# Attention scores with K's low half stored for every kv head on both partition halves

## The chip, the cores and the metric

The kernel runs on one core of a Trainium2 chip. The metric is the device time of one execution in microseconds (us), lower is better. The profile is that of one execution, taken by the hardware profiler; its times count from the start of its span.

## The reference

One transformer layer, on 1024 tokens of width 1024, in fp32: a norm, sliding-window attention with a sink, an output projection, a second norm, a gated feed-forward of width 2816, a final norm. The attention has 16 query heads in 4 groups; each group of 4 shares one kv head of 64 numbers.

```python
def sliding_window_sink_attention(h, w_in, sinks, w_out):
    B, T, _ = h.shape
    L = SWA_BLOCK                                   # 128 queries, 256 keys
    q, k, v = split_qkv(h, w_in)                    # 16, 4 and 4 heads of 64
    qb = q.reshape(B, nb, L, N_KV_HEADS, GQA_GROUP, HEAD_DIM)
    kw, vw = with_prev(k), with_prev(v)             # own block and the one before
    s = jnp.einsum('bnqhgd,bnkhd->bnhgqk', qb, kw) * (HEAD_DIM ** -0.5)
    s = s - slopes[:, :, None, None] * dist
    s = jnp.where(mask, s, -jnp.inf)
    m = jnp.maximum(jnp.max(s, axis=-1, keepdims=True), sink)
    p = jnp.exp(s - m)
    denom = jnp.sum(p, axis=-1, keepdims=True) + jnp.exp(sink - m)
    o = jnp.einsum('bnhgqk,bnkhd->bnqhgd', p / denom, vw)
    return o.reshape(B, T, ATTN_Q_DIM).astype(h.dtype) @ w_out

x = x + swa(rms_norm(x, norm_mix));  x = x + swiglu_ffn(rms_norm(x, norm_ffn), ...)
return rms_norm(x, final_norm)
```

## The kernel before

TensorE multiplies in fp32r. To keep fp32's precision each operand is split into a high part (a rounded copy, made on ScalarE) and a low part (the rest, by a subtraction on VectorE or GpSimd), and a product is made of three: high by high, high by low, low by high. `split` (L58) writes both parts; the class `Weights` loads each weight tile into one of 3 `raw` buffers, splits it into one of 3 `wc` buffers, and loads the next when a `raw` buffer comes free. Its two instructions have the lines L60 and L63 wherever they are called.

The order of every engine's instructions is written out by hand; the framework adds the waits. The stages are these:

1. Norm and V (L313 to L430): 8 tiles of 128 tokens are normed and transposed into H; V is projected as `pv` (L370). Its weights come as two raw halves that `wv_hi` and `wv_lo` split. In between, the first two K projections start.
2. K and Q of the first 512 tokens: ten products `pc` of 24 matmuls each (L265). `evac` of the two K products writes the high part KH for kv head 2i+par on the 64 partitions of par, and a DMA (L296) copies it to the other 64, so that KH stands on both halves. The low part KL (L295) stands once, two kv heads to a tile, each on its own half. Q's high and low parts go through DRAM into `qt`: for an even kv head the high part on partitions 0 to 63 and the low part on 64 to 127, for an odd one the other way round.
3. Attention: 32 units, one for each block n of 128 queries and each kv head. `att_iter` runs four units in a pipeline, a stage each: `scores` of unit i, `transpose` and `split_p` of unit i-1, `values` and `store_hi` of unit i-2, `store_lo` of unit i-3. Between these pieces it runs steps of a stream of plain matmuls: K and Q of the second 512 tokens for units 0 to 15 (15 a unit), the output projection `mo` of the first 512 (L612, 12 a unit) for units 16 to 31.
4. The output projection of the second half, the second norm with its row `wbc` (the norm's weights on every partition), and from 414 us the feed-forward.

A unit's scores are 8 matmuls, two for each of the 4 query heads, in pairs of this form (L480 to L483):

```python
nc.tensor.matmul(ps[:, i], self.qt[:, g], KH[:, kv, win], start=True, stop=False)
nc.tensor.matmul(
    ps[:, i], self.qt[self.rows, g], KL[self.rows, self.p, win], start=False, stop=True
)
```

The first contracts over 128 partitions (both Q parts by KH), the second over the 64 of `self.rows` (Q's high part by KL). VectorE then adds the bias and takes the row maximum (L488, four times; L492 negates two maxima at a time), ScalarE takes the exponentials (L497), GpSimd scales by the reciprocal of L508 (L510, four times), TensorE transposes (L519), ScalarE and VectorE split the transposed probabilities (`pr`, L60 and L63), TensorE multiplies by V (L533), and VectorE writes the low part of the result (L550, L551). All of a unit's PSUM tiles come from one pool of 4.

Of the kernel before, what the change touches and what calls it, by code (L numbers as in the profile page):

```python
# [9 lines left out]
F32 = mybir.dt.float32  # L10
F32R = mybir.dt.float32r
# [5 lines left out]
P = 128  # L17
# [15 lines left out]
def trunk_kernel(  # L33
# [21 lines left out]
    def f(ap):  # L55
        return ap.bitcast(F32)
# [14 lines left out]

    ident = const.tile([P, P], F32, name="ident")
    small = const.tile([P, 2 + NH], F32, name="small")
    wbc = const.tile([P, D], F32, name="wbc")
    sink_bc = small[:, 2:]
    H = [hpool.tile([P, 2, 2, NK, 2 * P], F32R, name=f"H{i}") for i in range(2)]
    q_dram = [[dram.tile([P, 4, G, P], F32, name=f"qs_{i}_{kv}") for kv in range(NKV)] for i in range(2)]
# [51 lines left out]
                lo = slot[:, 1, 4 * b : 4 * b + 4, off : off + P]  # L129
                split(hi, lo, self.pts[b], nc.scalar, nc.vector)  # L130

    # ------------------------------------------------- weights, split ahead of use
    class Weights:
        def __init__(self):
            self.jobs, self.nl, self.ns, self.lo = [], 0, 0, {}
# [92 lines left out]
            add_gu(c + 2)  # L228
            add_gu(c + 3)

    # ------------------------------------------------------------ matmul streams
    class Stream:
        def __init__(self, gen):
            self.gen, self.late, self.done = gen, [], False
# [38 lines left out]
    kvpool_cm = tc.tile_pool(name="kvpool", bufs=1)  # L273
    kvpool = kvpool_cm.__enter__()
    KH = kvpool.tile([P, NKV, T], F32R, name="KH")
    KL = kvpool.tile([P, 2, T], F32R, name="KL")
    VV = kvpool.tile([P, NT, 2, 4, HD], F32R, name="VV")
    qs_cm = tc.tile_pool(name="qs", bufs=2, side="right")
    qs = qs_cm.__enter__()
# [1 line left out]
    def qkv_steps(half):  # L281
        for i in range(10):
            ts_ = slice(half * 512, half * 512 + 512)
            j = half * 10 + i
            wc = W.get(j)
            ps = psg.tile([P, 512], F32, tag="g", name=f"pc_{half}_{i}")

            def evac(i=i, ps=ps, ts_=ts_):
                if i < 2:
                    for par in range(2):  # L290
                        r = slice(par * HD, par * HD + HD)
                        r2 = slice((1 - par) * HD, (1 - par) * HD + HD)
                        kv = 2 * i + par
                        nc.scalar.activation(KH[r, kv, ts_], ps[r], AF.Copy)
                        nc.vector.tensor_tensor(KL[r, i, ts_], ps[r], f(KH[r, kv, ts_]), ALU.subtract)  # L295
                        nc.sync.dma_start(f(KH[r2, kv, ts_]), f(KH[r, kv, ts_]))  # L296
                    return
                kv, gp = (i - 2) // 2, (i - 2) % 2
                qst = qs.tile([P, 2, 4, P], F32R, tag="qst", name=f"qst_{half}_{i}")
                pv = ps.rearrange("p (n q) -> p n q", n=4)  # L300
                nc.scalar.activation(qst[:, 0], pv, AF.Copy, scale=HD**-0.5)
                nc.vector.scalar_tensor_tensor(qst[:, 1], pv, HD**-0.5, f(qst[:, 0]), ALU.mult, ALU.subtract)
                for gi in range(2):
                    src = f(qst[gi * HD : (gi + 1) * HD])
                    for hl in range(2):
                        row = hl if kv % 2 == 0 else 1 - hl
                        dst = q_dram[half][kv][row * HD : (row + 1) * HD, :, gp * 2 + gi]
                        nc.sync.dma_start(dst, src[:, hl])

            yield from gemm_steps(ps, wc, half, lambda j=j: W.want(j + 3), evac)  # L310

    # ------------------------------------------------------- norm, V, first half
    early_cm = tc.tile_pool(name="early", bufs=1)  # L313
    early = early_cm.__enter__()
    manual = tc.manual_schedule()
# [4 lines left out]
    def load_x(t):  # L320
        xts[t] = early.tile([P, D], F32, tag="x", name=f"x_{t}", bufs=4)
        nc.sync.dma_start(xts[t], x[t * P : (t + 1) * P, :])

    row = early.tile([1, D], F32, name="row")
    srow = early.tile([1, NH], F32, name="srow")
    wv = early.tile([P, 2, NK, 256], F32R, name="wv")
    wv_raw = early.tile([P, NK, 256], F32, name="wv_raw")

    def load_wv(k2):
        nc.sync.dma_start(  # L330
            wv_raw[:, 4 * k2 : 4 * k2 + 4],
            w_in[k2 * 512 : k2 * 512 + 512, 1280:1536].rearrange("(k p) n -> p k n", p=P),
        )

# [17 lines left out]

    def wv_hi(k2):
        s = slice(4 * k2, 4 * k2 + 4)
        nc.scalar.activation(wv[:, 0, s], wv_raw[:, s], AF.Copy)

    def wv_lo(k2, eng):
        s = slice(4 * k2, 4 * k2 + 4)
        eng.tensor_tensor(wv[:, 1, s], wv_raw[:, s], f(wv[:, 0, s]), ALU.subtract)

    vps = {}

# [23 lines left out]
        norms[t].scale(**k)  # L386

    n_scale(0, halves=True)
    nc.vector.tensor_copy(wv[:, 0, :4], wv_raw[:, :4])
    norms[0].apply(parts=2)  # L390
    load_x(4)
    norms[0].transpose()
# [36 lines left out]
        v_evac(t)  # L429
    early_cm.__exit__(None, None, None)  # L430

    # ---------------------------------------------------------------- attention
    att_cm = tc.tile_pool(name="att", bufs=2)
    att = att_cm.__enter__()
    bias = att.tile([P, NH, 2 * P], F32, name="bias", bufs=1)
# [19 lines left out]
    class Unit:  # L455
# [12 lines left out]
        def scores(self):  # L468
            n, kv, b0, key = self.n, self.kv, self.b0, self.key
            w0 = max(n - 1, 0) * P  # L470
            win = slice(w0, w0 + 2 * P)
            nw = 2 * P - b0
            self.tt = att.tile([P, G, 2 * P], F32, tag="t", name=f"t_{key}", bufs=3)
            self.st = att.tile([P, 6, G], F32, tag="st", name=f"st_{key}", bufs=4)
            st = self.st
            for gp in range(2):
                ps = psa.tile([P, 2, 2 * P], F32, tag="a", name=f"s_{key}_{gp}")
                for i in range(2):
                    g = gp * 2 + i
                    nc.tensor.matmul(ps[:, i], self.qt[:, g], KH[:, kv, win], start=True, stop=False)  # L480
                    nc.tensor.matmul(  # L481
                        ps[:, i], self.qt[self.rows, g], KL[self.rows, self.p, win], start=False, stop=True
                    )  # L483
                gs = slice(gp * 2, gp * 2 + 2)
                for i in range(2):
                    g = gp * 2 + i
                    h = kv * G + g
                    nc.vector.tensor_tensor_reduce(  # L488
                        self.tt[:, g, b0:], ps[:, i, :nw], bias[:, h, b0:], scale=1.0,
                        scalar=sink_bc[:, h : h + 1], op0=ALU.add, op1=ALU.max, accum_out=st[:, 0, g : g + 1],  # L490
                    )
                nc.vector.tensor_scalar(st[:, 1, gs], st[:, 0, gs], -1.0, None, ALU.mult)  # L492
# [53 lines left out]
        def store_lo(self):  # L546
            slot = o_slot(self.n, self.p)
            rows, orow = self.rows, self.orow
            ot = att.tile([P, G, P], F32, tag="ot", name=f"ot_{self.key}", bufs=2)
            nc.vector.tensor_tensor(ot[rows], self.po[rows], f(slot[rows, 0]), ALU.subtract)  # L550
            nc.vector.tensor_tensor(slot[rows, 1], ot[rows], self.po[orow], ALU.add)  # L551

# [138 lines left out]
    s3 = Stream(out1_steps())  # L691
    for i in range(32, 35):
        att_iter(i, s3, 12)
    nc.sync.dma_start(wbc, norm_ffn[0].partition_broadcast(P))
    x2_cm.__exit__(None, None, None)
    att_cm.__exit__(None, None, None)
    kvpool_cm.__exit__(None, None, None)

    # ------------------------------------- output projection of the second half
    accp = ctx.enter_context(tc.tile_pool(name="accp", bufs=1))  # L700
    acc = [accp.tile([P, D], F32, name=f"acc_{t}") for t in range(NT)]
    xp = ctx.enter_context(tc.tile_pool(name="xp", bufs=2))
    actp = ctx.enter_context(tc.tile_pool(name="actp", bufs=3))
    wo1_cm = tc.tile_pool(name="wo1", bufs=1)
# [18 lines left out]
    s3.finish()  # L723
    wo1_cm.__exit__(None, None, None)

    # -------------------------------------------------------------------- ffn
    dnp = ctx.enter_context(tc.tile_pool(name="dnp", bufs=2))
    acts, gps = {}, {}

# [147 lines left out]
```

## Time and profile before

| | |
|---|---|
| Time, median of 3 runs | 1137.02 us (1136.62 to 1139.21) |
| Span of the profiled execution | 1136.2 us |
| TensorE busy | 1100.1 us, 97% |
| VectorE busy | 524.1 us, 46% |
| ScalarE busy | 345.9 us, 30% |
| GpSimd busy | 174.8 us, 15% |
| Attention, units 0 to 31 (scores of the first to scores of the last) | 114.6 to 341.5 us |
| Feed-forward | from 414 us to the end |

The profiled execution has no time of its own beside its span. The span lies 0.8 us under the median of the runs, and 0.4 us under the fastest: what lies around it is taken as that. A busy TensorE is one that has a matmul in flight, so 97% does not say that it works at its peak; how far apart the matmuls start does.

### The profile page before, as it was taken

The page shows a single profiled execution, that of the slowest core. Times are in us where ns is not written, and L with a number is a line of the kernel's source. Part 1 is how long each engine was busy: PE and PEld are TensorE (multiplying, and loading weights), DVE is VectorE, ACT ScalarE, POOL GpSimd, SP SyncE. Part 2 cuts the span into 40 slices and gives each one's busy share as a digit, 9 for nine tenths or more (in the row PEclk, how much of TensorE's full clock was granted, in tenths as well). Part 3 has the DMA queues.
Part 4 walks back from the last instruction along what each step waited for, and adds up shares of the span by engine and source line. Part 5 has one row for each costly group of instructions (what it writes and reads, how often), then busy time and mean ns, then how long its engine had stood idle before and what let it go on. Part 6 is the DMA issues. An engine that isn't in the chain of part 4 may idle for free.

```text
span 1136.2 us, 13051 instructions
## 1 busy us (share of the span) xinstructions
PE 1100.1 (97%) x4992; PEld 891.9 (79%) x4992; DVE 524.1 (46%) x978; ACT 345.9 (30%) x703; POOL 174.8 (15%) x260
## 2 busy tenths in 40 slices
PE   3999999999999899999999999999999999999997
PEld 2988777777777778888888888888888888888885
DVE  2544577777876634342524333242423334252427
ACT  2532566566664533111120212112020211111016
POOL 2357344444442100000000000000000000000002
PEclk6999999999999999999999999999999999999999
DMA  5257544543436613121120212121030212103003
GB/s 185 93 132 200 129 116 110 128 118 109 118 87 179 173 37 111 37 60 53 33 61 19 76 36 74 37 56 46 11 93 19 75 37 56 56 4 90 1 1 148
DMA packets 104305, 91.02 MB, mean 80 GB/s; under 512 B 4275, under 2 KB 87219, under 8 KB 104244
## 3 DMA queue, kind: packets, MB, share of 16 engines
q1 hardware_dynamic: 102946, 85.74, 27.2%
q10 hardware_dynamic: 1298, 4.46, 1.2%
q8 instruction: 39, 0.64, 0.2%
q14 instruction: 22, 0.18, 0.0%
HBM read 74.45 MB, written 14.68 MB: 78 GB/s over the span
## 4 chain that ended last, share of the span: by engine, by line
PE 93%; DMA 2%; issue 1%; ACT 1%; DVE 1%; POOL 0%; POOLq 0%; SPq 0%; ACTq 0%
PE gu L265 42%; PE d L821 21%; PE pc L265 10%; PE mo L612 5%; PE s L481 3%; PE s L480 3%; PE po L533 2%; PE pt L519 2%; DMA acc<-x2s 2%; PE pv L370 2%; PE mo L673 1%; PE pt_a L122 1%; PE pt_b L122 1%; DMA wv_raw<-in_swa_w_in_dram 0%; DVE xn_a L112 0%
## 5 line engine op out<-in xcount | busy, mean ns | idle before, releaser
L265 PE MATMUL gu<-H,wc_gu 128*128 128x512 f32 x2112 | 481.3, 389 | 0.0
L265 PEld LDWEIGHTS gu<-H,wc_gu 128*128 128x128 f32 x2112 | 396.3, 188 | 82.8
L821 PE MATMUL d<-wc_dn,act 128*128 128x512 f32 x1056 | 241.7, 390 | 0.0
L821 PEld LDWEIGHTS d<-wc_dn,act 128*128 128x128 f32 x1056 | 198.2, 188 | 41.7
L833 DVE TENSOR_TENSOR acc<-d,acc 128x512 f32<-128x512 f32 x176 | 121.6, 691 | 97.5 <-PE d L821 96.5
L63 DVE TENSOR_TENSOR wc_gu<-raw_gu,wc_gu 128x1024 fp32r<-128x1024 f32 x44 | 53.8, 1223 | 185.5 <-ACT wc_gu L60 185.5
L265 PE MATMUL pc<-H,wc_c 128*128 128x512 f32 x480 | 122.8, 399 | 2.2 <-POOL wc_c L63 2.2
L785 POOL TENSOR_SCALAR ssq_f<-ssq_f 128x1 f32<-128x1 f32 x7 | 1.3, 192 | 710.7 <-ACT sq L784 710.7
L265 PEld LDWEIGHTS pc<-H,wc_c 128*128 128x128 f32 x480 | 87.0, 188 | 21.6 <-POOL wc_c L63 2.6
L745 DVE TENSOR_TENSOR sil<-sil,gu 128x512 f32<-128x512 f32 x44 | 30.3, 688 | 136.7 <-PE gu L265 136.7
L60 ACT ACTIVATE act<-sil 128x512 fp32r<-128x512 f32 x44 | 27.8, 633 | 201.6 <-DVE sil L745 201.6
L497 ACT ACTIVATE t<-t,st 128x256 f32<-128x256 f32 (+1 forms) x128 | 62.4, 488 | 72.4 <-DVE st L492 72.3
L60 ACT ACTIVATE wc_dn<-raw_dn 128x1024 fp32r<-128x1024 f32 x22 | 22.1, 1051 | 197.7 <-PE d L821 197.7
L612 PE MATMUL mo<-wc_o,H 128*128 128x512 f32 x288 | 78.8, 405 | 0.0
L741 ACT ACTIVATE sil<-gu 128x512 f32<-128x512 f32 x44 | 26.4, 599 | 168.5 <-PE gu L265 168.5
L488 DVE CUSTOM_DVE_ANT_0 t<-s,bias,small 128x256 f32<-128x256 f32 (+1 forms) x128 | 54.6, 463 | 32.7 <-PE s L481 32.2
L510 POOL TENSOR_SCALAR t<-t,st 128x256 f32<-128x256 f32 (+1 forms) x128 | 57.6, 471 | 56.6 <-DVE st L508 26.5
L612 PEld LDWEIGHTS mo<-wc_o,H 128*128 128x128 f32 x288 | 51.4, 188 | 11.8 <-DVE xh L641 0.4
L63 POOL TENSOR_TENSOR wc_c<-raw_c,wc_c 128x1024 fp32r<-128x1024 f32 x20 | 48.1, 2407 | 26.6 <-ACT wc_c L60 19.4
L481 PE MATMUL s<-KL,qt 64*128 64x256 f32 x128 | 48.7, 380 | 0.0
L60 ACT ACTIVATE wc_gu<-raw_gu 128x1024 fp32r<-128x1024 f32 x44 | 46.1, 1048 | 8.4 <-issue 8.4
L63 DVE TENSOR_TENSOR pr<-pt,pr 128x512 fp32r<-128x512 f32 x60 | 41.0, 688 | 12.3 <-ACT pr L60 10.8
(96 smaller groups left out, 857.8 us busy)
## 6 DMA issues: line engine op xcount, KB each, us to landing
raw_gu<-in_ffn_w_gate_up_dram SPq DMA_DIRECT2D x44, 512.0 KB, 5.0
raw_dn<-in_ffn_w_down_dram SPq DMA_DIRECT2D x22, 512.0 KB, 3.4
raw_c<-in_swa_w_in_dram SPq DMA_DIRECT2D x20, 512.0 KB, 4.0
qs<-qst SPq DMA_DIRECT2D x64, 128.0 KB, 2.5
qt<-qs SPq DMA_DIRECT2D x32, 256.0 KB, 4.0
raw_o<-in_swa_w_out_dram SPq DMA_DIRECT2D x24, 256.0 KB, 3.8
x<-in_x_dram SPq DMA_DIRECT2D x8, 512.0 KB, 3.5
out_dram<-acc SPq DMA_DIRECT2D x7, 512.0 KB, 2.6
```

The lines of the kernel that those rows point to most:

```text
L60: nc.scalar.activation(hi, src, AF.Copy)
L63: lo_eng.tensor_tensor(lo, src, f(hi), ALU.subtract)
L265: nc.tensor.matmul(ps, wc[:, wl, k], hh[:, :, hl, k, :], start=(n == 0), stop=(n == 3 * NK - 1))
L480: nc.tensor.matmul(ps[:, i], self.qt[:, g], KH[:, kv, win], start=True, stop=False)
L481: nc.tensor.matmul(ps[:, i], self.qt[self.rows, g], KL[self.rows, self.p, win], start=False, stop=True)
L488: nc.vector.tensor_tensor_reduce(self.tt[:, g, b0:], ps[:, i, :nw], bias[:, h, b0:], scale=1.0, scalar=sink_bc[:, h : h + 1], op0=ALU.add, ...
L497: nc.scalar.activation(self.tt[:, g, b0:], self.tt[:, g, b0:], AF.Exp, bias=st[:, 1, g : g + 1], accum_out=st[:, 3, g : g + 1],)
L510: nc.gpsimd.tensor_scalar(self.tt[:, g, b0:], self.tt[:, g, b0:], st[:, 2, g : g + 1], 0.0, ALU.mult, ALU.add)
L612: nc.tensor.matmul(pss[i], o[:, a, g], wt[:, b, ci], start=(c == 0 and n % 3 == 0), stop=(c == 7 and n % 3 == 2))
L745: nc.vector.tensor_tensor(sil, sil, ps, ALU.mult)
L821: nc.tensor.matmul(ps, acts[c][:, a, t * P : (t + 1) * P], dnw[c][:, b, s], start=(n == 0), stop=(n == 3 * len(cs) - 1),)
L833: nc.vector.tensor_tensor(acc[t][:, s], ps, acc[t][:, s], ALU.add)
```

## The change

The low part of K gets the layout that the high part has: `KL` holds all four kv heads, and a second DMA copies each piece to the other 64 partitions. The second matmul of each pair then contracts over 128 partitions; Q's low part by KL, which was left out, is added to the scores. `KL` doubles, so three buffers move: the norm row `wbc` becomes two tiles in pools that live shorter, `ot` has one buffer in place of two, and V's raw weights share the three `raw` buffers of the weight tiles.

```diff
@@ -71,7 +71,6 @@
-    wbc = const.tile([P, D], F32, name="wbc")
@@ -273,7 +272,7 @@
-    KL = kvpool.tile([P, 2, T], F32R, name="KL")
+    KL = kvpool.tile([P, NKV, T], F32R, name="KL")
@@ -292,8 +291,9 @@
                         nc.scalar.activation(KH[r, kv, ts_], ps[r], AF.Copy)
-                        nc.vector.tensor_tensor(KL[r, i, ts_], ps[r], f(KH[r, kv, ts_]), ALU.subtract)
+                        nc.vector.tensor_tensor(KL[r, kv, ts_], ps[r], f(KH[r, kv, ts_]), ALU.subtract)
                         nc.sync.dma_start(f(KH[r2, kv, ts_]), f(KH[r, kv, ts_]))
+                        nc.sync.dma_start(f(KL[r2, kv, ts_]), f(KL[r, kv, ts_]))
@@ -321,14 +321,15 @@
+    wbc = early.tile([P, D], F32, name="wbc_mix")
     row = early.tile([1, D], F32, name="row")
     srow = early.tile([1, NH], F32, name="srow")
     wv = early.tile([P, 2, NK, 256], F32R, name="wv")
-    wv_raw = early.tile([P, NK, 256], F32, name="wv_raw")
+    wv_raw = [wp.tile([P, 4, 256], F32, tag="raw", name=f"wv_raw_{i}", bufs=3) for i in range(2)]
@@ -478,9 +479,7 @@
                     nc.tensor.matmul(ps[:, i], self.qt[:, g], KH[:, kv, win], start=True, stop=False)
-                    nc.tensor.matmul(
-                        ps[:, i], self.qt[self.rows, g], KL[self.rows, self.p, win], start=False, stop=True
-                    )
+                    nc.tensor.matmul(ps[:, i], self.qt[:, g], KL[:, kv, win], start=False, stop=True)
@@ -546,7 +545,7 @@
-            ot = att.tile([P, G, P], F32, tag="ot", name=f"ot_{self.key}", bufs=2)
+            ot = att.tile([P, G, P], F32, tag="ot", name=f"ot_{self.key}", bufs=1)
@@ -691,14 +690,15 @@
-    nc.sync.dma_start(wbc, norm_ffn[0].partition_broadcast(P))
     x2_cm.__exit__(None, None, None)
     att_cm.__exit__(None, None, None)
     kvpool_cm.__exit__(None, None, None)
@@
     acc = [accp.tile([P, D], F32, name=f"acc_{t}") for t in range(NT)]
+    wbc = accp.tile([P, D], F32, name="wbc_ffn")
+    nc.sync.dma_start(wbc, norm_ffn[0].partition_broadcast(P))
```

On TensorE, VectorE, ScalarE and GpSimd the instructions stand in the same order as before; the queue of SyncE (SP), which issues most DMAs, gets eight more. Two places show it. A row gives the line, what is written and read, the size, and in brackets what the instruction waits for: engines by name, earlier DMAs as DMAHW.

The first place is the start of the program on SP: the loads of the first K weights (`raw_c`) and of the token tiles 4 to 7 (`x`). Before:

```order
L173 DMA raw_c_0_119<-in_swa_w_in_dram 128x8x128 [waits DMAHW0_49]
L173 DMA raw_c_1_121<-in_swa_w_in_dram 128x8x128 [waits DMAHW1_49]
L173 DMA raw_c_2_123<-in_swa_w_in_dram 128x8x128 [waits DMAHW2_49]
L322 DMA x_166<-in_x_dram 128x1024 [waits DMAHW3_49,DVE_49,Activation_49]
L322 DMA x_190<-in_x_dram 128x1024 [waits DMAHW4_49,DVE_49,Activation_49]
```

And with the change:

```order
L172 DMA raw_c_0_120<-in_swa_w_in_dram 128x8x128 [waits DMAHW0_49]
L172 DMA raw_c_1_122<-in_swa_w_in_dram 128x8x128 [waits DMAHW2_49,DMAHW1_49,Pool_49]
L172 DMA raw_c_2_124<-in_swa_w_in_dram 128x8x128 [waits DMAHW4_49,DVE_49]
L322 DMA x_167<-in_x_dram 128x1024 [waits DMAHW3_49]
L322 DMA x_191<-in_x_dram 128x1024
```

No row moved, but two of the three weight loads now wait for the engines that split V's raw weights (`wv_lo`, L359: first GpSimd, then VectorE), and the two token tiles stand behind them.

The second place is further on in the same queue, where the first K products are copied to the other partition half. Before:

```order
L173 DMA raw_c_5_401<-in_swa_w_in_dram 128x8x128 [waits DMAHW2_49,Pool_49]
L296 DMA KH<-KH 64x512 [waits Activation_49]
L296 DMA KH<-KH 64x512 [waits DMAHW3_49,Activation_49]
L173 DMA raw_c_6_486<-in_swa_w_in_dram 128x8x128 [waits DMAHW7_49,DMAHW4_49,Pool_49]
L296 DMA KH<-KH 64x512 [waits DMAHW5_49,Activation_49]
```

And with the change:

```order
L172 DMA raw_c_5_402<-in_swa_w_in_dram 128x8x128 [waits DMAHW2_49,Pool_49]
L295 DMA KH<-KH 64x512 [waits Activation_49]
L296 DMA KL<-KL 64x512 [waits DMAHW3_49,DVE_49]
L295 DMA KH<-KH 64x512 [waits DMAHW4_49,Activation_49]
L296 DMA KL<-KL 64x512 [waits DMAHW5_49,DVE_49]
L172 DMA raw_c_6_489<-in_swa_w_in_dram 128x8x128 [waits DMAHW7_49,DMAHW6_49,Pool_49]
```

Behind each copy of KH stands one of KL, which waits for VectorE's subtraction.

## Rows read from the trace of the kernel before

**Rows 1.** Windows: us, busy (instructions) of PE, PEld, DVE, ACT, POOL; PEclk, DMA.

```profile
113.00:235.00 122.00, 122.00 (x536) 89.70 (x534) 82.64 (x258) 72.32 (x207) 54.66 (x91) 1.00 0.49 118
235.00:346.00 111.00, 111.00 (x505) 82.27 (x505) 86.85 (x261) 68.77 (x199) 48.58 (x86) 1.00 0.38 106
```

**Rows 2.** The page, part 4: the chain that ended last, by engine.

```profile
PE 93%; DMA 2%; issue 1%; ACT 1%; DVE 1%; POOL 0%; POOLq 0%; SPq 0%; ACTq 0%
```

**Rows 3.** Timeline of PE, one unit's scores: start, duration (us), engine, line, operation.

```profile
303.60 0.28 PE L480 MATMUL s<-KH,qt 128*128 128x256 f32 x1
303.81 0.38 PE L481 MATMUL s<-KL,qt 64*128 64x256 f32 x1
304.12 0.38 PE L480 MATMUL s<-KH,qt 128*128 128x256 f32 x1
...
305.99 0.50 PE L612 MATMUL mo<-wc_o,H 128*128 128x512 f32 x1
```

**Rows 4.** Timeline of PEld (weight loads) in the same unit.

```profile
304.11 0.19 PEld L480 LDWEIGHTS s<-KH,qt 128*128 128x128 f32 x1
```

**Rows 5.** Timeline of PE, one tile's V projection and what follows it.

```profile
61.53 2.99 PE L370 MATMUL pv<-wv,H 128*128 128x256 f32 x24
64.35 0.39 PE L265 MATMUL pc<-H,wc_c 128*128 128x512 f32 x1
```

**Rows 6.** Tile pv: its weight loads, ns min/median/max.

```profile
L370 PEld LDWEIGHTS pv<-wv,H x192: 187/188/333, 26.2 to 84.4; 128*128 128x128 f32 x192
```

**Rows 7.** Timeline of all engines: VectorE and GpSimd around the start of that unit.

```profile
304.09 2.37 POOL L63 TENSOR_TENSOR wc_o<-raw_o,wc_o 128x1024 fp32r<-128x1024 f32 x1 [0.23 <-ACT wc_o L60]
...
304.85 0.48 DVE L488 CUSTOM_DVE_ANT_0 t<-s,bias,small 128x256 f32<-128x256 f32 x1 [1.06 <-PE s L481]
...
305.78 0.71 DVE L492 TENSOR_SCALAR st<-st 128x2 f32<-128x2 f32 x1
```

**Rows 8.** Line L492, the negated maxima: ns min/median/max.

```profile
L492 DVE TENSOR_SCALAR st<-st x64: 168/169/1357, 116.7 to 342.5; 128x2 f32<-128x2 f32 x64
```

**Rows 9.** VectorE's waits from 113 to 235: us in total, times, longest.

```profile
DVE t L488 <- PE s L481: 16.5, 19, 2.4
```

**Rows 10.** VectorE's waits from 235 to 346.

```profile
DVE t L488 <- PE s L481: 15.7, 21, 1.1
```

**Rows 11.** GpSimd's lines from 113 to 235: busy, mean ns, idle before, releaser.

```profile
L63 POOL TENSOR_TENSOR wc_c<-raw_c,wc_c 128x1024 fp32r<-128x1024 f32 x9 | 21.4, 2374 | 2.8 <-ACT wc_c L60 2.8
L63 POOL TENSOR_TENSOR wc_o<-raw_o,wc_o 128x1024 fp32r<-128x1024 f32 x2 | 4.7, 2358 | 0.7 <-ACT wc_o L60 0.7
```

**Rows 12.** GpSimd's lines from 235 to 346.

```profile
L63 POOL TENSOR_TENSOR wc_o<-raw_o,wc_o 128x1024 fp32r<-128x1024 f32 x8 | 18.9, 2366 | 2.1 <-ACT wc_o L60 2.1
```

**Rows 13.** Timeline of all engines after the attention.

```profile
355.63 0.58 SPq L694 DMA_DIRECT2D wbc<-in_norm_ffn_dram  x1
...
365.17 1.28 DVE L112 SCALAR_TENSOR_TENSOR xn_b<-acc,ssq_b,wbc 128x1024 f32<-128x1024 f32 x1 [5.87 <-DMA wbc<-in_norm_ffn_dram]
...
366.61 1.06 PE L122 MATMUL pt_b<-ident,xn_b 128*128 128x128 f32 x8 [1.34 <-DVE xn_b L112]
...
380.93 1.94 PE L122 MATMUL pt_b<-ident,xn_b 128*128 128x128 f32 x8 [3.10 <-DVE xn_b L112]
```

**Rows 14.** Windows: the stretch behind that last wait.

```profile
380.73:384.14 3.41, 3.21 (x12) 2.95 (x13) 3.41 (x6) 1.53 (x3) 0.00 (x0) 0.50 0.42 139
```

**Rows 15.** Timeline of all engines, the first stage.

```profile
28.84 1.22 DVE L359 TENSOR_TENSOR wv<-wv_raw,wv 128x1024 fp32r<-128x1024 f32 x1
...
35.11 1.06 ACT L103 ACTIVATE xn_a<-x 128x1024 f32<-128x1024 f32 x1
...
61.34 0.59 SPq L296 DMA_DIRECT2D KH<-KH  x1
```

**Rows 16.** DMA issues up to 120 us: KB each, median us to landing.

```profile
x<-in_x_dram SPq DMA_DIRECT2D x8, 512.0 KB, 3.5
...
KH<-KH SPq DMA_DIRECT2D x4, 128.0 KB, 4.3
```

More of the change, by code (lines that the diff above doesn't have):

```diff
@@ L326, in trunk_kernel @@
     wv = early.tile([P, 2, NK, 256], F32R, name="wv")
-    wv_raw = early.tile([P, NK, 256], F32, name="wv_raw")
+    wv_raw = [wp.tile([P, 4, 256], F32, tag="raw", name=f"wv_raw_{i}", bufs=3) for i in range(2)]
     def load_wv(k2):
         nc.sync.dma_start(
-            wv_raw[:, 4 * k2 : 4 * k2 + 4],
+            wv_raw[k2],
             w_in[k2 * 512 : k2 * 512 + 512, 1280:1536].rearrange("(k p) n -> p k n", p=P),
@@ L354, in wv_hi @@
         s = slice(4 * k2, 4 * k2 + 4)
-        nc.scalar.activation(wv[:, 0, s], wv_raw[:, s], AF.Copy)
+        nc.scalar.activation(wv[:, 0, s], wv_raw[k2], AF.Copy)
     def wv_lo(k2, eng):
         s = slice(4 * k2, 4 * k2 + 4)
-        eng.tensor_tensor(wv[:, 1, s], wv_raw[:, s], f(wv[:, 0, s]), ALU.subtract)
+        eng.tensor_tensor(wv[:, 1, s], wv_raw[k2], f(wv[:, 0, s]), ALU.subtract)
     vps = {}
@@ L388, in trunk_kernel @@
     n_scale(0, halves=True)
-    nc.vector.tensor_copy(wv[:, 0, :4], wv_raw[:, :4])
+    nc.vector.tensor_copy(wv[:, 0, :4], wv_raw[0])
     norms[0].apply(parts=2)
```

## The prediction

> **What bounds the kernel now.** I read the chain that ended last first: 93% of it is TensorE (PE) [rows 2]. The change touches the score matmuls, so the second view is the windows over the attention, cut where the stream of plain matmuls changes from K and Q to the output projection [rows 1]. In both stretches PE always has a matmul in flight, at a granted clock of 1.00, while VectorE (DVE) is busy for 82.64 of 122 us and 86.85 of 111 us. So PE sets the pace, but DVE is not far behind: a PE that needs a quarter less would meet it. The third view is the timeline of PE in one unit, because "in flight" does not say how fast matmuls follow each other [rows 3].
>
> **The score matmuls.** The eight matmuls of a unit take from 303.60 to 305.99, 2.39 us. After a matmul on 128 rows the one on 64 starts 0.21 later (303.60 to 303.81); the next one, on 128 rows again, starts 0.31 later (303.81 to 304.12), and the rest keep that step [rows 3]. Its weight load starts at 304.11, at the moment of its own matmul and not ahead of it [rows 4]. What does the same shape cost when all 128 rows are used every time? The trace has it: `pv` multiplies 128x128 by 128x256, the new form exactly, and its 24 matmuls run from 61.53 to 64.35 in 2.82 us, 0.118 us each [rows 5]. Their weight loads last 188 ns at the median [rows 6], longer than the step, so they must lie beside other matmuls. The step of 0.31 is then a price of the change between 128 and 64 rows, not of the load.
>
> With the change a bundle takes 8 x 0.118 = 0.94 us in place of 2.39: 1.45 less, and over 32 units 46.4 us less of PE. The multiplications that are added (64 more rows) cost nothing by the same row. The bounds for a bundle are 0.94 (as `pv`) and 2.39 (nothing gained). I take 0.94, since shape, type and order of loads are the same.
>
> The Trainium skill, "TensorE: Matmul & The Clock Gate", Part 3, says that a weight load runs beside matmuls in flight only if its row group differs from theirs. By it two matmuls on all 128 rows would load and multiply in turn and the gain would be nothing, where by the rows on `pv` it is 46.4 on PE; those rows speak against the rule, and it stands below as a rival.
>
> **What takes PE's place.** The 46.4 is a gain on PE alone. Stretch 1 (113 to 235) has 17 of the bundles, stretch 2 (235 to 346) 15. PE's floor is 122 - 17 x 1.45 = 97.4 and 111 - 15 x 1.45 = 89.3.
>
> DVE's floor starts from its busy time, 82.64 and 86.85. It idles 39.4 and 24.2, of which 16.5 and 15.7 are waits for the scores [rows 9, 10]; these go when PE is faster. The other idle time, 22.9 and 8.45, is in short waits for ScalarE and others within the pipeline.
>
> DVE's busy time does not stay, however. The negation L492 normally takes 169 ns, but up to 1357 [rows 8]. In the unit shown it takes 0.71 and ends at 306.49, just as GpSimd's split of a weight tile ends (304.09 + 2.37 = 306.46) [rows 7]. It seems held until the other engine finishes. The first reduction L488 starts at 304.85 after DVE idled 1.06 for the scores. Without that idle time L492 is due about 1.06 earlier while the split ends when it did, so it is held some 1.1 to 1.2 longer, and part of the gain is eaten. I take 1.2 for each split: 11 of them in stretch 1 (9 + 2), 8 in stretch 2 [rows 11, 12]. DVE's floor becomes 82.64 + 13.2 = 95.8 and 86.85 + 9.6 = 96.5.
>
> For stretch 1 the new length lies between 97.4 (PE's floor; DVE's is just below) and 95.8 + 22.9 = 118.7 (all other idle time kept): a gain of 3.3 to 24.6. Two engines that both are within two per cent of full can't both run without gaps; I keep a third of DVE's other idle time, 7.6, which is my choice: 103.4, a gain of 18.6. For stretch 2 the bounds are 96.5 and 104.9, a gain of 6.1 to 14.5; with a third, 2.8, it is 99.3, a gain of 11.7. If the hold on L492 does not bite, the bounds there reach PE's 89.3, a gain of 21.8.
>
> **The hand-over behind the attention.** Today PE runs late and everything else is ready. Later PE reaches the end of the attention closer to DVE, and the second norm hangs on DVE: it waits 5.87 for `wbc`, whose load is issued at 355.63, and PE waits 1.34 and then 3.10 for DVE's `xn_b` [rows 13]. What PE gained beyond the others is given back here. With four PSUM tiles PE can lead by about a unit, 233 / 32 = 7.3 us. The bounds are 0 and 7.3; I take half, 3.6.
>
> **The edits that I cost at nothing.** The eight copies of KL: SP issues a KH copy at 61.34 in 0.59 us [rows 15], so the two that follow the first K products add some 1.2 us each time to SP's queue, and a copy lands 4.3 us after its issue [rows 16]; the first scores start at 114.6. For the second half the copy of a piece runs while eight products of Q are still to come. Without that cover a copy would cost its 4.3 once in each half. V's raw weights in `raw`: the third weight load now waits for DVE's L359, which ends at 28.84 + 1.22 = 30.06 [rows 15], and token tiles 4 and 5 stand behind it in SP. Three or four issues and a landing of 3.5 us [rows 16] put tile 4 at about 34 to 36, and ScalarE reads it at 35.11 [rows 15]: 0 to 1 us late on ScalarE, and I take 0, as only the norm's next step, some microseconds on, feeds PE. If tile 4 came a whole landing later, 3.5 would be the loss. `ot` with one buffer: its writer L550 and its reader L551 follow each other on DVE, in order, so nothing waits that did not. `wbc` as two tiles: the second load now also waits for PE's last reader of the old space, the attention's last values, which are before 355.63, so nothing moves; a microsecond if not.
>
> **The sum.** The profiled execution's span is 1136.2, 0.8 below the median, and I put the differences on the median: 1137.0 - 18.6 - 11.7 + 3.6 = 1110.3. I say 1110.
>
> **The rivals.**
>
> *PE stays the only bound.* L492 is not held longer, and DVE's other waits close up. Then both stretches shrink to PE's floors: 1137.0 - 46.4 = 1090.6, up to about 1099 with the hand-over. For it: much of DVE's idle time is waiting that a new rhythm could fill. Against it: in stretch 2 DVE is busy for 86.85, against PE's 89.3, and the held L492 is plain [rows 1, 7]. Chance 0.14.
>
> *DVE takes over, with all its other waits.* The gain is 3.3 + 6.1 = 9.4, less up to 3.6 for the hand-over: 1127.6 to 1131. For it: the waits are on ScalarE's and GpSimd's work in the same chain, which is not shortened by the change. Against it: a chain over four units has slack, and a wait is shorter when DVE comes late. Chance 0.18.
>
> *The step stays at 0.31.* If the load of a 128-row matmul can't start while another one on the same rows runs, nothing is gained: load and multiplication in line take 0.19 + 0.12 = 0.31, just the step that is seen [rows 3, 4]. Then the change only swaps 0.31 for 0.31: 1137. Against it: `pv` loads and multiplies in the same way at 0.118 [rows 5, 6]. Chance 0.05. This is the rule of the Trainium skill, "TensorE: Matmul & The Clock Gate", Part 3, that was weighed above.
>
> *Slower: the clock falls in the attention.* Today PE never waits there. After the wait of 3.10 before 380.93 the granted clock in the next 3.41 us is 0.50, that is 1.2 GHz in place of 2.4 [rows 13, 14]. A PE that waits for DVE in every unit might be granted less. One such stretch does 1.7 us of full-speed work in 3.41, so it costs 1.7; with 26.7 to lose it takes 16 of them, one in every second unit, to be back at 1137, and one in each unit gives 1137 - 26.7 + 32 x 1.7 = 1165. For it: DVE's floor is close to or above PE's, so waits will come. Against it: the waits I expect sum to 6.0 (103.4 - 97.4) and 10.0 (99.3 - 89.3) us, half a microsecond a unit, well below the wait of 3.10, and single waits should stay short. Chance 0.05, most of it slower, a part within 0.3%.
>
> **How the numbers follow.** The forecast, both engines near their floors with some gaps, has a chance of 0.58 and spans 1100 to 1120. With PE alone at 1091 to 1099 (0.14) and DVE with all its waits at 1120 to 1131 (0.18) that is 0.90. The range of 1094 to 1129 leaves out 0.10 for no gain or a loss, and about 0.04 at either end of the neighbouring cases, 0.18 together. About 0.3%, 3.4 us, is what a measurement of this kernel can tell from no change. Faster by more: 0.58 + 0.14 + 0.18 = 0.90, and a little from the bundle between its bounds, 0.91; within: 0.05; slower: 0.04.
>
> **What would show it.** In the timeline of PE the score matmuls should start 0.12 apart, with weight loads ahead of their matmuls. PE should no longer be busy for 100% of the two stretches, and its waits should name DVE or the PSUM tiles that DVE frees. DVE's wait for scores should fall from 32 us to under 10, the sum of L492 should rise by some 20 us, and the stretches should measure about 103 and 99 us. The granted clock should stay at 1.00 in both. If steps of 0.31 remain, the first step is wrong; if L492's sum does not grow, the second; if PE's waits are there but behind ScalarE or GpSimd, the choice of a third. The prediction would be wrong as a whole if the clock fell in the attention, or if the start (first scores at 114.6) moved by more than a microsecond.

## The result and the profile after

The changed kernel takes 1106.43 us (median of 4 runs, 1105.46 to 1109.92) against 1137.17 us before: a ratio of 0.9734, 95% interval 0.9716 to 0.9752, 30.7 us less. The forecast was 1110, in the likeliest case, 1100 to 1120. The profiled execution has a span of 1103.7 us, 32.5 below the 1136.2 of before and somewhat more than the medians differ by.

The line of the page on the chain that ended last, by engine, shows VectorE where it had 1% before [rows 2]:

```profile
PE 81%; DVE 11%; ACT 3%; DMA 2%; issue 2%; POOL 0%; SPq 0%; POOLq 0%; DVEq 0%; ACTq 0%
```

The timeline of PE and of its weight loads (PEld) at the first bundle of scores answers to [rows 3, 4]. Both score matmuls have 128 rows, they start 0.12 apart, and a load starts with the matmul before the one that it is for:

```profile
113.57 0.28 PE L481 MATMUL s<-KH,qt 128*128 128x256 f32 x1
113.57 0.19 PEld L482 LDWEIGHTS s<-KL,qt 128*128 128x128 f32 x1
113.68 0.28 PE L482 MATMUL s<-KL,qt 128*128 128x256 f32 x1
113.69 0.19 PEld L481 LDWEIGHTS s<-KH,qt 128*128 128x128 f32 x1
113.80 0.28 PE L481 MATMUL s<-KH,qt 128*128 128x256 f32 x1
```

The windows, cut at the first scores, the first `mo`, the end of the last scores, the first `mo` of `wc_wo` and the first matmul of the feed-forward, which starts at 375.1 us here and at 407.7 in the kernel before, not at the 414 of the table ahead (the columns are those of [rows 1]):

```profile
113.60:216.70 103.10, 97.83 (x530) 80.71 (x529) 89.53 (x256) 69.55 (x206) 52.00 (x89) 1.00 0.60 143
216.70:310.30 93.60, 87.27 (x483) 71.51 (x482) 87.12 (x246) 63.54 (x189) 48.99 (x83) 1.00 0.45 124
310.30:342.60 32.30, 31.37 (x154) 25.40 (x152) 21.62 (x38) 16.40 (x30) 8.91 (x13) 1.00 0.72 196
342.60:375.10 32.50, 29.03 (x136) 23.08 (x137) 20.72 (x26) 14.47 (x24) 3.69 (x10) 0.95 0.44 130
```

The same cuts of the kernel before, taken for this comparison, are:

```profile
114.60:235.10 120.50, 120.50 (x530) 88.43 (x528) 82.74 (x258) 72.32 (x207) 54.40 (x90) 1.00 0.49 118
235.10:341.50 106.40, 106.40 (x482) 78.45 (x481) 82.55 (x249) 65.08 (x188) 47.53 (x83) 1.00 0.39 109
341.50:375.20 33.70, 31.80 (x153) 25.49 (x152) 20.89 (x33) 16.66 (x30) 8.31 (x11) 1.00 0.73 198
375.20:407.70 32.50, 29.03 (x138) 23.45 (x138) 20.80 (x26) 14.63 (x24) 3.70 (x10) 0.95 0.39 119
```

The differences are 17.4 in the first half of the attention, 12.8 in the second, 1.4 in the hand-over and nothing in the stage behind it; 1.0 lies ahead of the first scores. PE now waits: it is busy for 97.83 of 103.10 and 87.27 of 93.60 us. The waits in the first half whose last releaser is VectorE (total, times, longest) name the PSUM tiles that VectorE frees by L487, the reduction of the scores, and by its split of `pr`; VectorE hardly waits for scores any more, 1.0 us where it was 16.5 [rows 9] (the last row, from VectorE's own waits) and 1.8 in the second half, where it was 15.7 [rows 10]:

```profile
PE po L532 <- DVE st L487: 2.3, 4, 0.8
...
PE s L481 <- DVE pr L63: 1.2, 2, 0.9
...
DVE t L487 <- PE s L482: 1.0, 3, 0.5
```

The negation, now L491, has the same median as in [rows 8] and a longer tail, up to 2404 ns. Grouped by line its sum is 34.8 us, where it was 17.7:

```profile
L491 DVE TENSOR_SCALAR st<-st x64: 168/170/2404, 115.7 to 312.0; 128x2 f32<-128x2 f32 x64
```

The timeline of one unit shows what [rows 7] showed, larger. GpSimd splits a weight tile from 253.67 to 256.05. The first pair of reductions runs through it at its usual duration; the negation behind it starts at 254.42 and ends at 256.08; only then comes the second pair, which frees the other tile of scores:

```profile
253.67 2.38 POOL L63 TENSOR_TENSOR wc_o<-raw_o,wc_o 128x1024 fp32r<-128x1024 f32 x1
...
253.89 0.48 DVE L487 CUSTOM_DVE_ANT_0 t<-s,bias,small 128x256 f32<-128x256 f32 x1
254.30 0.08 DVE L487 DVE_READ_ACCUMULATOR2_ANT st<- 128x1 f32 x1
254.42 1.66 DVE L491 TENSOR_SCALAR st<-st 128x2 f32<-128x2 f32 x1
...
255.99 0.47 DVE L487 CUSTOM_DVE_ANT_0 t<-s,bias,small 128x256 f32<-128x256 f32 x1
```

Fourteen of the 64 negations are stretched so, as before, and every one ends 0.02 to 0.03 us after a split of GpSimd does.

### The profile page after: what moved, and what is told of

It reads as the page before. It is cut to its first block, busy times and chain, and to the rows that moved or that the text cites. A ratio compares the mean times of both kernels' runs of the same rounds, so it can differ in the third digit from the quotient of the medians.

```text
span 1103.7 us, 13070 instructions
## 1 busy us (share of the span) xinstructions
PE 1057.8 (96%) x4992; PEld 876.8 (79%) x4992; DVE 536.3 (49%) x978; ACT 341.2 (31%) x703; POOL 174.4 (16%) x260
## 4 chain that ended last, share of the span: by engine, by line
PE 81%; DVE 11%; ACT 3%; DMA 2%; issue 2%; POOL 0%; SPq 0%; POOLq 0%; DVEq 0%; ACTq 0%
PE gu L264 43%; PE d L821 21%; PE pc L264 7%; DVE t L487 3%; DVE st L491 3%; PE mo L611 2%; PE pv L371 2%; PE po L532 1%; DMA raw_wo<-in_swa_w_out_dram 1%; DVE pr L63 1%; PE pt L518 1%; PE mo L672 1%; DVE ot L549 1%; PE s L481 1%; PE pt_a L121 1%
## 5 line engine op out<-in xcount | busy, mean ns | idle before, releaser
L487 DVE CUSTOM_DVE_ANT_0 t<-s,bias,small 128x256 f32<-128x256 f32 (+1 forms) x128 | 54.3, 461 | 3.0 <-PE s L482 2.8
L60 ACT ACTIVATE wc_gu<-raw_gu 128x1024 fp32r<-128x1024 f32 x44 | 46.1, 1048 | 8.4 <-issue 8.4
L63 DVE TENSOR_TENSOR act<-sil,act 128x512 fp32r<-128x512 f32 x44 | 30.5, 693 | 30.8 <-ACT act L60 30.8
L532 PE MATMUL po<-pr,VV 128*128 128x512 f32 x120 | 33.9, 401 | 5.9 <-DVE st L487 5.8
```

What stands on the lines that cost most here:

```text
L60: nc.scalar.activation(hi, src, AF.Copy)
L63: lo_eng.tensor_tensor(lo, src, f(hi), ALU.subtract)
L487: nc.vector.tensor_tensor_reduce(self.tt[:, g, b0:], ps[:, i, :nw], bias[:, h, b0:], scale=1.0, scalar=sink_bc[:, h : h + 1], op0=ALU.add, ...
L532: nc.tensor.matmul(self.po, VV[:, blk, self.p].rearrange("p (a b) d -> p a b d", a=2)[:, self.par], pr[:, hl], start=(cnt == 0), stop=(cnt ...
```

## The experiments

Twelve kernels were run, each against the kernel before. The theory is that the gain is the step of the score matmuls alone, and that what is missing to PE's 46.4 us is the negation held by GpSimd's splits. The rivals are that buffers or copies carry part of it, that a 64-row matmul is slow in itself, and that VectorE's other waits set the new pace.

| run | what it is | median us | ratio (95%) |
|---|---|---|---|
| moves_only | the buffers move, KL as before | 1137.06 | 0.9994 (0.998 to 1.0008) |
| copied_64 | KL copied, its matmuls on 64 rows | 1137.76 | 1.0003 (0.9989 to 1.0018) |
| half_128 | 128 rows for two heads of four | 1113.42 | 0.9791 (0.9773 to 0.9809) |
| order_64 | 64 rows, half as many changes of rows | 1113.75 | 0.9795 (0.9771 to 0.9818) |
| neg_tt | changed, negation as two-tensor operation | 1107.57 | 0.974 (0.9725 to 0.9755) |
| split_dve | changed, GpSimd's splits on VectorE | 1103.12 | 0.9697 (0.9678 to 0.9716) |
| neg_act | changed, negation on ScalarE | 1095.73 | 0.964 (0.9625 to 0.9655) |
| before_neg_act | before, negation on ScalarE | 1137.02 | 1.0004 (0.999 to 1.0018) |
| neg_reduce | changed, negation as a reduction | 1094.71 | 0.9624 (0.9605 to 0.9643) |
| neg_act_qt | neg_act, Q loaded a unit earlier | 1092.89 | 0.9607 (0.9593 to 0.9621) |
| qt_ahead | changed, Q loaded a unit earlier | 1106.90 | 0.9728 (0.9712 to 0.9744) |
| neg_reduce_qt | neg_reduce, Q loaded a unit earlier | 1090.43 | 0.9589 (0.9574 to 0.9604) |

**Is it the matmul?** Run moves_only is the changed kernel with KL and its matmul as they were:

```diff
-    KL = kvpool.tile([P, NKV, T], F32R, name="KL")
+    KL = kvpool.tile([P, 2, T], F32R, name="KL")
...
-                        nc.sync.dma_start(f(KL[r2, kv, ts_]), f(KL[r, kv, ts_]))
...
-                    nc.tensor.matmul(ps[:, i], self.qt[:, g], KL[:, kv, win], start=False, stop=True)
+                    nc.tensor.matmul(
+                        ps[:, i], self.qt[self.rows, g], KL[self.rows, self.p, win], start=False, stop=True
+                    )
```

> Only the three buffers move; KL stands once and its matmuls use 64 rows, as in the kernel before. Theory (the gain is TensorE's steps in the scores): 1135.5 to 1138, bundles of 2.39 us. Rival (a good part of the gain comes from the buffers: the earlier load of the norm row, the weight loads that no longer crowd the start): 1133 or less, with the first transpose near 23.5 us where it was at 24.4, and the second norm's wait for its row near 3.4 where it was 5.9.

Run copied_64 keeps the doubled KL and its copies, and only the matmul reads 64 rows, `KL[self.rows, kv, win]`; the multiplication of Q's low part by KL falls away with it.

> The whole change with KL on both halves and its copies, but the second matmul of each pair contracts over 64 rows again. Theory (the form of the matmul is the gain, copies and buffers cost nothing): the same time as with the buffers alone within 1 us, 1135.5 to 1138, bundles of 2.39 us. Rival (layout or copies carry part of it): below 1133 or above 1140.

Neither differs from the kernel before: 1137.06 and 1137.76. So the buffers, the eight copies and the doubled tile give and cost nothing that can be measured, and the form of the matmul is the whole gain. The 1.0 us at the start is a difference between executions: the first scores of moves_only start at 115.2 and of copied_64 at 114.8, with the changed buffers, and at 114.6 and 113.6 in the kernels before and after.

**How much for half of it?** Run half_128 uses the new form for the first two heads of a unit:

```diff
-                    nc.tensor.matmul(ps[:, i], self.qt[:, g], KL[:, kv, win], start=False, stop=True)
+                    rr = slice(0, P) if gp == 0 else self.rows
+                    nc.tensor.matmul(ps[:, i], self.qt[rr, g], KL[rr, kv, win], start=False, stop=True)
```

> The change for two of the four heads of each unit; the other two keep 64 rows. On TensorE a bundle should take 0.47 + 0.21 + 3 x 0.31 = 1.61 us, 0.78 less than before, 25 us over 32 units. Theory (the whole change is cut off because VectorE becomes the bound, half of it is not): most of the gain is there already, 1110 to 1115. Rival (each 128-row matmul is worth the same, what is missing to 46 us lies elsewhere on TensorE): half of the gain of 30.7, about 1121 to 1123.

It takes 1113.42, 24 us less, about all of the 25 that PE was to save. The second half of the change, another 21 us on PE by the prediction's count, brings only 7: the gain is cut off, as the theory says.

**Is it the change of rows, or the 64 rows?** Run order_64 goes back to 64 rows for KL, but puts KL's matmul first for every second head, so that equal forms stand next to each other:

```diff
-                    nc.tensor.matmul(ps[:, i], self.qt[:, g], KH[:, kv, win], start=True, stop=False)
-                    nc.tensor.matmul(ps[:, i], self.qt[:, g], KL[:, kv, win], start=False, stop=True)
+                    both = [(slice(0, P), KH), (self.rows, KL)]
+                    for m, (rr, kk) in enumerate(both if i == 0 else both[::-1]):
+                        nc.tensor.matmul(
+                            ps[:, i], self.qt[rr, g], kk[rr, kv, win], start=(m == 0), stop=(m == 1)
+                        )
```

> The changed kernel, but KL's matmuls contract over 64 rows again, and for every second head they stand ahead of KH's, so that in a unit there are four changes between 128 and 64 rows where there were eight. Theory (the change of rows is what costs): four steps of 0.31 (the first 0.21) and four of 0.12, 1.6 us a bundle, 1110 to 1117. Rival (a 64-row matmul is slow in itself, or a load can't run beside a matmul on the same rows): bundles of 2.2 to 2.4 us, 1132 to 1138.

The timeline of PE in one bundle, where x2 is two matmuls of one form:

```profile
254.15 0.28 PE L483 MATMUL s<-KH,qt 128*128 128x256 f32 x1
254.35 0.50 PE L483 MATMUL s<-KL,qt 64*128 64x256 f32 x2
254.78 0.50 PE L483 MATMUL s<-KH,qt 128*128 128x256 f32 x2
255.22 0.50 PE L483 MATMUL s<-KL,qt 64*128 64x256 f32 x2
255.64 0.39 PE L483 MATMUL s<-KH,qt 128*128 128x256 f32 x1
255.87 0.39 PE L614 MATMUL mo<-wc_o,H 128*128 128x512 f32 x1
```

A bundle takes 1.72 us (255.87 - 254.15), where it was 2.39, and the time is 1113.75, with as many 64-row matmuls as before. By their starts the steps are not the 0.12 and 0.31 that I expected: two of one form take 0.43, and all eight steps of the unit shown are 0.20 to 0.22. A matmul behind a change is recorded from the start of its own weight load, as in [rows 4], and some 0.10 longer. So is the plain matmul behind the bundle in the kernel before: it takes 0.50 [rows 3], where it takes 0.39 here. The price of a change is therefore better read from the first score to the second plain matmul behind the bundle. Its rows, for the units shown of the kernel before, of order_64 and of the changed kernel, are:

```profile
306.33 0.39 PE L612 MATMUL mo<-wc_o,H 128*128 128x512 f32 x1
...
256.10 0.39 PE L614 MATMUL mo<-wc_o,H 128*128 128x512 f32 x1
...
114.75 0.40 PE L264 MATMUL pc<-H,wc_c 128*128 128x512 f32 x1
```

That makes 2.73 us with eight changes (306.33 - 303.60), 1.95 with four (256.10 - 254.15) and 1.18 with none (114.75 - 113.57). half_128, which has four changes as well but two 64-row matmuls a unit in place of four, takes 1.96 (the median of its units), and nearly the same time, 1113.42. So a change costs about 0.19 us, and a 64-row matmul is not slow in itself. The rival that the load can't run beside a matmul on the same rows is out: 128 after 128 goes at 0.12 with loads of 0.19. The price is about as long as one weight load; whether it is that load alone the runs don't separate.

**Is it the hold?** Run neg_tt gives the negation another form, zero minus the maximum, with the zeros in SBUF:

```diff
...
-                nc.vector.tensor_scalar(st[:, 1, gs], st[:, 0, gs], -1.0, None, ALU.mult)
+                nc.vector.tensor_tensor(st[:, 1, gs], small[:, 2 + NH :], st[:, 0, gs], ALU.subtract)
```

> The changed kernel, with the negation of the row maxima written as zero minus maximum by a two-tensor operation in place of the one-tensor operation with a constant. Theory (the negation is held until a GpSimd split of weights ends, and that is what keeps the attention above TensorE's floor): its sum falls from 34.8 to about 11 us, TensorE's waits in the two stretches (5.3 and 6.3 us) shrink to half or less, 1096 to 1102. Rival 1 (any small VectorE instruction at this place is held): sum and time stay, 1105 to 1108. Rival 2 (the hold goes, but VectorE's other waits in the pipeline keep the pace): sum near 11, time within 2 us of 1106.

This missed: 1107.57. The row of the line shows that the new form is held just the same:

```profile
L492 DVE TENSOR_TENSOR st<-small,st x64: 160/161/2395, 117.7 to 313.8; 128x2 f32<-128x2 f32 x64
```

What I had expected of this form was wrong; whether the hold is the limit was still open. Run split_dve takes away what holds: the low halves of the weights `c1` and `o0`, split during the attention, are subtracted on VectorE.

```diff
-            W.add(f"c{half}_{i}", [NK, P], cols(w_in, c0), nc.gpsimd)
+            W.add(f"c{half}_{i}", [NK, P], cols(w_in, c0), nc.vector if half else nc.gpsimd)
...
-            add_wo(f"o0{nh}", c, nh, nc.gpsimd)
+            add_wo(f"o0{nh}", c, nh, nc.vector)
```

> The changed kernel, with the low halves of the weights that are split during the attention subtracted on VectorE in place of GpSimd. Theory (GpSimd's splits hold VectorE's negation): its 64 instructions fall to 0.17 us each, 11 us in all, though its form and place are unchanged; VectorE gets some 19 splits of 1.2 us, about what the holds took, so the time stays near: 1102 to 1112. Rival (something else at this place stretches it): its sum stays above 30 us.

The same negation, at the same place, is back at a mean of 196 ns. One is still stretched, to 1.91 us, and it lies under a split that GpSimd kept:

```profile
L491 DVE TENSOR_SCALAR st<-st 128x2 f32<-128x2 f32 x64 | 12.6, 196 | 2.2
```

So GpSimd's splits are the cause. The time, 1103.12, is only 3.3 us better; VectorE now has 16 splits, 20.2 us of work, where it had the holds.

**What is the hold worth?** Run neg_act moves the negation to ScalarE, so that no VectorE instruction stands there:

```diff
-                nc.vector.tensor_scalar(st[:, 1, gs], st[:, 0, gs], -1.0, None, ALU.mult)
...
             for g in range(G):
+                if g % 2 == 0:
+                    gs = slice(g, g + 2)
+                    nc.scalar.activation(st[:, 1, gs], st[:, 0, gs], AF.Copy, scale=-1.0)
```

> The changed kernel, with the negation of the row maxima moved from VectorE to ScalarE, ahead of the exponentials that use it. Theory (a VectorE instruction with all its operands in SBUF is held while GpSimd splits a weight tile; it stands between two reductions that read the scores and so keeps PSUM tiles from TensorE): no VectorE instruction between 113 and 310 us lasts over 1 us, TensorE's waits in the two stretches (11.6 us together) at least halve, 1097 to 1102. Rival 1 (the hold passes on to another SBUF instruction of VectorE): a new group of 1.5 to 2.4 us durations, 1104 to 1108. Rival 2 (VectorE's other work and ScalarE keep the pace; ScalarE gets 64 more instructions of some 0.2 us): 1105 to 1112.

1095.73, 10.7 us under the changed kernel and a little better than expected. No VectorE instruction of the units is stretched. The same edit in the kernel before is the control:

> The kernel before, with the negation moved to ScalarE in the same way. Theory (TensorE alone bounds the attention there, so VectorE's holds are hidden): the holds go and the time stays, 1135 to 1139. Rival (part of VectorE's waits is already on the path): 1134 or less.

1137.02, no change: as long as PE was the bound, the holds were hidden. They became a cost only by the change.

**Which instructions are held?** In neg_act's expectation I had put it down to all operands being in SBUF. Run neg_reduce tests that: the negation is on VectorE again, from SBUF to SBUF, as a reduction over one element.

```diff
-                nc.vector.tensor_scalar(st[:, 1, gs], st[:, 0, gs], -1.0, None, ALU.mult)
+                nc.vector.tensor_reduce(
+                    st[:, 1, gs], st[:, 0, gs].rearrange("p (g o) -> p g o", o=1),
+                    mybir.AxisListType.X, ALU.max, negate=True,
+                )
```

> The changed kernel, with the negation as a reduction over one element that negates its result, on VectorE at the same place, from SBUF to SBUF. Theory A (only some forms are held: one tensor by a constant, and two tensors of SBUF, as measured, but not a reduction): no duration over 0.3 us, the time as with ScalarE or a little under it since ScalarE is not charged, 1093 to 1098. Theory B (every VectorE instruction with all its operands in SBUF is held): the sum stays above 30 us, 1104 to 1108. The Trainium skill, SBUF (State Buffer), has A: by its rules on the pair of ports that VectorE and GpSimd share, a reduction never contends on this chip.

Theory A holds, and my own earlier wording (theory B) falls: no instance lasts longer than 157 ns, though 22 of the 64 lie wholly within splits, and the time is 1094.71.

```profile
L491 DVE TENSOR_REDUCE st<-st x64: 154/154/157, 118.4 to 302.6; 128x2 f32<-128x2 f32 x64
```

The Trainium skill, "SBUF — State Buffer", Who interferes with whom, says that VectorE and GpSimd share one pair of SBUF ports, which one of them holds for a whole instruction; that `tensor_scalar` can contend for the pair in its two-port form, and `tensor_tensor` with both inputs in SBUF with a GpSimd instruction that reads SBUF; and that a reduction on trn2 never contends. The runs agree, though none shows which form a `tensor_scalar` took: 34.8 us in the changed kernel and 33.7 between 113 and 310 us in neg_tt, against 9.9 with the reduction.

**What is next?** In neg_act PE's longest waits were for Q. A row of the timeline of PE, and the windows from 243.70 to the end of that wait and of a stretch behind it:

```profile
245.89 0.36 PE L481 MATMUL s<-KH,qt 128*128 128x256 f32 x1 [2.15 <-DMA qt<-qs]
```

```profile
243.70:245.90 2.20, 0.05 (x2) 0.04 (x1) 0.40 (x1) 1.10 (x2) 2.20 (x4) 1.00 0.23 83
...
246.50:249.90 3.40, 3.40 (x15) 2.91 (x15) 3.08 (x10) 2.25 (x9) 0.82 (x2) 0.53 0.37 99
```

The load stood in SP's queue behind two weight loads, issued from 236.13, just after a split of GpSimd had ended (236.11), and three loads of tokens; it was issued only from 239.08 on. Behind the wait the granted clock is 0.53 for 3.4 us, mostly its lower level of 1.2 GHz. This is the fall of the clock of the prediction's slower rival, but behind a wait for a load and not for VectorE, and in a kernel that has come further. Runs neg_act_qt and qt_ahead load Q one unit earlier:

```diff
-            self.qt = att.tile([P, G, P], F32R, tag="qt", name=f"qt_{self.key}", bufs=3)
+            self.qt = att.tile([P, G, P], F32R, tag="qt", name=f"qt_{self.key}", bufs=4)
...
-        if i + 2 < 32:
-            units[i + 2].load()
+        if i == 0:
+            units[2].load()
+        if i + 3 < 32:
+            units[i + 3].load()
```

> The changed kernel with the negation on ScalarE, and each unit's Q loaded one unit earlier into a fourth buffer. In the run with the negation moved, TensorE waited 2.15 us for a Q load at 245.89 that stood in SyncE's queue behind weight loads, and the granted clock was 0.67 from 245 to 250; another wait of 1.45 was at 294.71. Theory (with the holds gone, these loads are the next wait, and the clock falls behind the longer one): no wait for Q loads, the clock 1.00 from 114 to 300, 3.6 us of waits and about 1.7 of slow clock less, 1089 to 1092.5. Rival (the loads only take the blame for a wait that VectorE would set anyway): 1094 to 1097.

> The changed kernel with Q loaded one unit earlier, the negation still on VectorE. Theory (there the holds set the pace, and the loads come in time): 1104 to 1108. Rival (the loads cost the changed kernel something too): 1102 or less.

neg_act_qt takes 1092.89, 2.8 us less than neg_act; that is a little above the range that I gave, though its attention went as the theory says: no wait for Q and a clock of 1.00 in both stretches. Its first scores start at 116.2, in neg_act at 114.3, which is part of the difference. qt_ahead takes 1106.90: with the holds in place earlier loads are worth nothing.

Run neg_reduce_qt has both, the reduction and the earlier loads.

> The same, with Q loaded one unit earlier into a fourth buffer. Theory A: no holds, no waits for Q, clock 1.00 through the attention: TensorE's floor there, 1089 to 1093. Theory B: as the changed kernel with Q loaded earlier, 1104 to 1108.

1090.43 us. The window over its whole attention:

```profile
114.40:295.20 180.80, 178.74 (x1010) 153.02 (x1009) 154.08 (x504) 134.33 (x394) 101.57 (x172) 1.00 0.57 146
```

180.8 us, where it was 226.9 before (114.6 to 341.5), 46.1 less; by the medians the gain is 46.45 (1136.88 - 1090.43). The 46.4 us that the prediction counted on PE have arrived. PE has a matmul in flight for 178.74 us of the attention, 48.2 less than before (120.50 + 106.40).

## Why the prediction was right, and where its terms were off

*The step.* "A bundle takes 8 x 0.118 = 0.94" is shown by the rows after; that it comes from the change of rows is shown by order_64 and half_128. The 46.4 us that it should free on PE are a little short: the count ends where the plain matmul behind the bundle starts, and before the change that one paid as well (0.50 us in [rows 3]). With it a unit saves 1.55 us (2.73 - 1.18), some 49 us over 32 units, an estimate from the units shown. In neg_reduce_qt PE's busy time in the attention fell by 48.2 and the attention's length by 46.1.

*The hold.* That VectorE takes PE's place through the held negation is shown by neg_act, neg_reduce and split_dve. The price was right and the count too high: the sum rose by 17.1 us (34.8 - 17.7), 1.2 for each of 14 holds, while I had charged 19 splits, 22.8. The rows of the two stretches count one split that began before the attention and one across their common end twice over; of the 17 that are left three held no negation, before the change and after it.

*The two halves.* 18.6 and 11.7 were forecast, 17.4 and 12.8 measured. That they are so close owes something to luck: in the first half VectorE's busy time is 6 us lower than the floor that I set (89.53 against 95.8), and its idle time 13.6 where I kept 7.6. I took VectorE to be near full; it isn't. The pace is set by when it frees a PSUM tile, which the hold delays, and it idles at other times. The choice of "a third of the other idle time" has no support in the runs.

*The hand-over.* I took a loss of 3.6; it was a gain of 1.4. The second norm's wait for its row fell from 5.87 to 3.4 us, as the load landed after 7.4 in place of 9.4 us. In moves_only, copied_64 and half_128 it landed after 9.1, 9.4 and 8.8 and VectorE waited 5.6, 5.7 and 5.2, so the buffer's place isn't the reason. Over all the kernels it lands after 6.9 to 9.8 us; why it varies was not tested, so the gain of 1.4 owes something to luck. The mechanism that I gave, PE's lead that is given back, is not seen even where PE hardly waits for VectorE: from the end of the last scores to the first matmul of the feed-forward it takes 64.6 us in neg_reduce_qt, 66.1 before and 64.8 with the change. This is the term that was mis-sized: of the 5.9 us by which the sum of the terms (26.7) fell short of the profiled executions' difference (32.6, by the cuts) it makes 5.0.

*The edits at nothing* were nothing (moves_only, copied_64).

*The rivals.* "PE stays the only bound" did not happen, but its time of 1090.6 is what neg_reduce_qt reached, by taking away the holds and the late loads of Q. "VectorE with all its other waits" did not happen: VectorE idled 13.6 and 6.5 us in the two halves, where the rival kept 22.9 and 8.45. "The step stays at 0.31", the rule of the Trainium skill, "TensorE: Matmul & The Clock Gate", Part 3, is refuted by the loads of the changed kernel, 0.19 long at steps of 0.12. The fall of the clock did not occur in the changed kernel (1.00 in all of the attention), where single waits stayed at 1.1 us and less; it occurred in the attention of neg_act, once, behind a wait of 2.15.

*What stays open:* where the 1 to 2 us come from by which the start differs between executions (the first scores lie between 113.6 and 116.5 us in these kernels), and what decides whether a wait lowers the clock: in neg_act the wait of 1.45 at 294.71 left it at 1.00, and so did PE's waits of 2.44 in half_128 and 2.71 in qt_ahead ahead of the second norm's transposes, both longer than the 2.15 behind which it fell. Nor do the runs show whether the price of a change of rows is the weight load alone.

## What to carry to other kernels

A matmul's step can be read off another place in the same trace that has the same shape; where it is longer at one place, look at what stands ahead of it, since here the alternation of 128 and 64 rows cost more than the multiplications it saved. The instruction behind the stretch can pay as well, so measure to the one after it. When the bound engine is relieved by a quarter, list which instructions of the next engine are stretched today under cover, for those holds grow when the cover goes: count the instances, don't take the number of possible ones. A held instruction of 0.17 us costs what is queued behind it, so its form or its engine is worth changing even if its sum looks small.

## What the runs showed of the hardware

Each change between matmuls of 64 and of 128 rows costs about 0.19 us here (2.73, 1.95 and 1.18 us a unit with eight, four and no changes), whether a unit has four 64-row matmuls (order_64, 1.95) or two (half_128, 1.96). Matmuls on 128 rows follow each other at 0.12 with weight loads of 0.19 us beside them. A VectorE instruction that negates two numbers a partition took up to 2.4 us while GpSimd subtracted two SBUF tiles, both as a tensor by a constant and as two tensors, and never more than 157 ns as a reduction. I had not expected that the form decides, nor that two tensors are held as one is.
